# Re-ranking the splitting of weights, and 24 remainders made by accumulating DMAs

## The chip, the cores and the metric

One core of one Trainium2 chip runs the whole program. The metric is the device time of one execution in microseconds (us). Of the kernel before, three executions took 697.01, 698.89 and 701.65 us, so the median is 698.89 us.

## The reference

Two decoder layers over 256 tokens of width 1024, in float32, and a final norm:

```
for layer in range(DEPTH):
    h = rms_norm(x, mix_norm[layer])
    if layer % 2 == 0:
        x = x + gdn_shortconv_mixer(h, ...)
    else:
        x = x + nsa_mixer(h, ...)
    x = x + squared_relu_mlp(rms_norm(x, mlp_norm[layer]), w_up[layer], w_down[layer])
return rms_norm(x, final_norm)
```

The first mixer projects `h` to q, k, v (each 512 wide, then a causal convolution of width 4 and SiLU), z, a, b and three short-convolution parts of 512 (b_gate, c_gate, hs). Its two outputs, the gated delta rule over chunks (`y_a`) and the gated convolution (`y_b`), go side by side into one output projection of 1024 x 1024. The second mixer is block-sparse attention. Each layer ends in an MLP of 1024 x 4096 x 1024.

## The kernel before

**Split weights.** Every large product is made of TensorE products in the type float32r. A weight `w` is split into a high part `uh` (ScalarE: a copy of `w` to float32r) and a remainder `ul = w - uh` (VectorE: a subtraction). Activations are split in the same way, and one tile of a product takes three matmuls: high x high, high x remainder, remainder x high (`mm256`). Weights come from HBM in slots `st` of 128 x 2048 (SyncE issues the loads; four slots). A slot holds two units of 128 x 1024; a unit takes 24 matmuls of 256 columns. There are four buffers each for `uh` and `ul`, so unit i can be split only when unit i-4 has been used. The function `splits` does it, as two streams, one for the even units and one for the odd. A slot is filled anew when both its units are split.

**Units.** Units 0 to 7 are the projection k, 8 to 15 are z, a and b (128 x 512 and 128 x 528), 16 to 19 v, 20 to 23 q, 24 to 27 c_gate, 28 to 31 hs, 32 to 35 b_gate, 36 to 43 the first mixer's output projection. The MLPs and the second mixer follow.

**The first mixer's chain.** After k is convolved (`preconv`, `cvconv`, `K` on VectorE), a chain of small steps follows: the norms of k (`s`, `rk`, `rqt`), `nbk`, `KB`, the scores `al`, the inversion of the chunk's triangle (`lc`, `tt`, `uc`, `ys`, TensorE and VectorE in turn), the two solves (`x`), the outputs (`o`, with GpSimd and ScalarE helping) and `ya`, the second half of the output projection's input. The other half is `yb`. TensorE does the units' matmuls between the steps of the chain. GpSimd makes the mask products `gt`, the convolution of q (`cvpool`, `tap`) and that of the short channel (`CG`).

**The order.** All operations are issued through a wrapper (line 294), so nearly every row of the profile bears L294; the DMA loads bear L426, and instructions are told apart by tile names. A planner written into the kernel (`Order`) simulates the engines with costs and picks at each step the stream that can start first; equal starts go by the stream's rank, the smaller first. A chain has rank 0 or 1, the main stream of matmuls 9, the splits `SPLIT`. What it picks becomes the fixed order of instructions on each engine. A wait in that order holds back what stands behind it on its engine.

Of the kernel before, what the change touches and what calls it, by code (L numbers as in the profile page):

```python
# [10 lines left out]
F32 = mybir.dt.float32  # L11
F32R = mybir.dt.float32r
# [20 lines left out]
PK, PW, PR, F1, GZ, ZP, LD, RT, P2 = 1, 0, 1, 1, 1, 1, 1, 21, 8  # L33
KPOOL, VPOOL, CVB = (), (), {'conv': 4, 'pool': 2}
CHAIN, TOK_FIRST = 0, False
TICK, BUSY = 10240 / 3, 1500.0
MAIN, SPLIT, SHARE, LIMIT, FLOOR, CAP, SPARE = 9, 0, 0.5, 300, -1500.0, 4000.0, 1
ORDER1 = ('kk', 'q0', 'kc', 'vg', 'cmp', 'q1', 'wo')


# [116 lines left out]
class Order:  # L157
# [28 lines left out]
    def flag(self, name):  # L186
        self.flags.setdefault(name, self._now())
# [14 lines left out]
    def spend(self, eng, cost, cols=0.0, port=False):  # L202
# [18 lines left out]
        self.free[eng] = c.t - self.OVER[eng]  # L221
        c.last = eng

    def _next(self, s, value):
        prev, self.cur = self.cur, s
        try:
            s.want = s.gen.send(value)
        except StopIteration:
            self.streams.remove(s)
        self.cur = prev  # L230
# [19 lines left out]
    def run(self):  # L250
        while self.streams:
            best = None
            for i, s in enumerate(self.streams):
                t, at = self._start(s)
                prio = -1 if s.prio == MAIN and self.debt > self.limit else s.prio
                if t is not None and (best is None or (t, prio, i) < best[0]):
                    best = (t, prio, i), s, at
            assert best, [s.want for s in self.streams]
            _, s, at = best
            w, value = s.want, None  # L260
            if isinstance(w, (str, dict)):
                value = at
            else:
                s.hold = max(s.hold, at)
                if w[0] == 'bank':
                    slot = min(self.banks)
                    self.banks.remove(slot)
                    value = self.get_bank(slot[1])
                    self.held[id(value)] = slot[1], value
                elif w[0] == 'take':  # L270
                    self.tokens[w[1]].remove(min(self.tokens[w[1]]))
            self._next(s, value)
# [11 lines left out]
class Timed:  # L284
# [14 lines left out]
    def cost(self, op, a, k):  # L299
        aps = [x for x in list(a) + list(k.values()) if isinstance(x, bass.AP)]  # L300
        size = lambda x: int(np.prod(x.shape[1:]))
        if self.name != 'PE':
            return self.other(op, a, k, aps, size)
        rows = aps[1].shape[0]
        if op == 'transpose':
            return 0.85 * rows, rows * rows / 128
        m, n = size(aps[1]), size(aps[2])
        if aps[2].dtype == F32:
            if m <= 64 and aps[0].start_partition():
                return 8 + 0.7 * m, 0.0  # L310
            return max(1.75 * m, 1.68 * n), 4 * n * rows / 128
        return max((0.86 if aps[2].dtype == F32R else 0.25) * m, 0.46 * n), n * rows / 128

    def other(self, op, a, k, aps, size):
        n = max(size(x) for x in aps)
        if 'dma' in op:
            return 60.0,
        col = any(size(x) == 1 for x in aps[2:]) and n > 1
        sbuf = sum(x.space != PSUM and size(x) > 1 for x in aps[1:])
        if self.name == 'V':  # L320
            if op == 'reciprocal':
                return 150 + 6.4 * n,
            if op == 'memset':
                return 58 + 0.8 * n, 0.0, True
            if op in ('tensor_copy', 'tensor_scalar'):
                quick = sbuf == 1 and aps[0].space != PSUM
                return 150 + (0.55 if quick else 1.06) * n + 60 * col, 0.0, quick
            return 155 + 1.05 * n + 60 * col, 0.0, sbuf > 1 and op not in ('transpose', 'stream_shuffle', 'tensor_reduce')
        if self.name == 'G':
            if op == 'memset':  # L330
                return 90 + 0.9 * n,
            if op in ('tensor_scalar', 'tensor_copy'):
                return 145 + 1.2 * n,
            col = any(list(x.ap)[-1][0] == 0 for x in aps)
            return 180 + (1.68 if col else 2.12) * n,
        need = TABLES.get(a[2] if op == 'activation' else None)
        swap = 0.0
        if need and self.order.table not in need:
            self.order.table, swap = need[0], 1283.0
        return (swap + (150 if aps[1].space == PSUM else 188) + 0.85 * n + 95 * isinstance(k.get('scale'), bass.AP)  # L340
                + 190 * ('accum_out' in k)),
# [26 lines left out]
def _build(ctx, nc, tc, wts, xin, parin, out, off):  # L368
# [86 lines left out]
    def splits(first):  # L455
        for i in range(first, len(units), 2):
# [7 lines left out]
            lo = unitp.tile([128, UN + 64], F32R, name=f"ul{i % UB}")[:, :UN]  # L464
            yield 'A'
            A.activation(hi[:, :n], src, AF.Copy)
            yield 'V'
            V.tensor_sub(lo[:, :n], src, hi[:, :n].bitcast(F32))
            made[i] = hi, lo
            slot = place[p][0]  # L470
            left[slot] -= 1
            if not left[slot]:
                flag(f'st{slot}')
            flag(f'u{i}')

    def unit(keep=1):

# [1383 lines left out]
```

## Time and profile before

| | |
|---|---|
| median of 3 executions | 698.89 us |
| the profiled execution | 699.36 us |
| its span, first to last instruction | 697.6 us |
| mean granted TensorE clock | 0.981 of full |
| TensorE busy (PE) | 664.7 us |
| VectorE busy (DVE) | 479.5 us |
| ScalarE busy (ACT) | 388.1 us |
| GpSimd busy (POOL) | 136.2 us |

PE is TensorE's matmuls, PEld its weight loads, SP the engine that issues loads. Matmuls are pipelined and their ends are modelled. PEclk is the granted clock of TensorE, 1.00 for 2.4 GHz and 0.50 for 1.2 GHz. The first mixer ends at some 180 us of the span.

### The profile page before, as it was taken

To read this page: it belongs to the slowest core of one execution; us is meant where nothing else is said; L and a number is where in the kernel's file an instruction comes from. 1 tells how busy PE (TensorE), PEld (TensorE's weight loads), DVE (VectorE), ACT (ScalarE), POOL (GpSimd) and SP (SyncE) were. 2 spreads that over 40 slices of the span, in tenths; PEclk is the share of its full clock that TensorE was granted. 3 is DMA by queue.
4 is the path that set the end of the run, shared out by engine and by line. 5 is a ranking of instruction groups with operands and counts; after the bars stand their busy time and mean duration, and the time that the engine had idled before them with its cause. 6 is when DMAs were issued, how large, how long until landed. Compare 5 with 4: busy or idle time off the path is not lost.

```text
span 697.6 us, 15854 instructions
## 1 busy us (share of the span) xinstructions
PE 664.7 (95%) x6573; PEld 625.0 (90%) x6573; DVE 479.5 (69%) x898; ACT 388.1 (56%) x750; POOL 136.2 (20%) x177
## 2 busy tenths in 40 slices
PE   8998879996999999999999999999899999999994
PEld 6997779996999999999999876978699999999994
DVE  6999868674775556566568999997396655555452
ACT  7556223331588787444446567676478878544430
POOL 2035678100210000011013251212130000011121
PEclk9999989997999999999999999999999999999997
DMA  8843331311355555555553367213135555555501
GB/s 296 289 175 136 122 123 64 107 36 55 138 206 190 183 189 203 209 185 182 190 207 110 129 224 290 73 62 122 61 122 182 183 183 195 207 201 182 182 1 60
DMA packets 17640, 109.05 MB, mean 156 GB/s; under 512 B 2080, under 2 KB 2336, under 8 KB 5536
## 3 DMA queue, kind: packets, MB, share of 16 engines
q1 hardware_dynamic: 17280, 107.52, 44.1%
q8 instruction: 51, 0.84, 0.5%
q10 hardware_dynamic: 288, 0.52, 0.2%
q14 instruction: 21, 0.17, 0.1%
HBM read 106.99 MB, written 1.05 MB: 155 GB/s over the span
## 4 chain that ended last, share of the span: by engine, by line
PE 75%; DVE 16%; issue 3%; ACT 3%; DMA 1%; SPq 0%; POOL 0%; DVEq 0%; ACTq 0%; POOLq 0%
PE b L294 75%; DVE ul L294 4%; DVE cvconv L294 1%; DVE x L294 1%; ACT uh L294 1%; DVE kc L294 1%; DMA X<-xt 1%; DVE swq L294 1%; DVE rqt L294 1%; DVE X L294 1%; DVE nm L294 0%; ACT px L294 0%; DVE lc L294 0%; DVE qr L294 0%; DVE cm L294 0%
## 5 line engine op out<-in xcount | busy, mean ns | idle before, releaser
L294 DVE TENSOR_TENSOR ul<-st,uh 128x1024 fp32r<-128x1024 f32 (+3 forms) x204 | 244.2, 1200 | 143.4 <-ACT uh L294 141.1
L294 ACT ACTIVATE uh<-st 128x1024 fp32r<-128x1024 f32 (+3 forms) x204 | 205.8, 1011 | 195.3 <-PE b L294 179.6
L294 PE MATMUL b<-x,uh 128*128 128x256 f32 (+1 forms) x1632 | 295.5, 283 | 2.0 <-DVE x L294 0.8
L294 PEld LDWEIGHTS b<-x,uh 128*128 128x128 f32 x1632 | 249.4, 189 | 6.6 <-ACT uh L294 1.8
L294 PE MATMUL b<-x,ul 128*128 128x256 f32 x832 | 231.1, 279 | 0.7 <-DVE ul L294 0.6
L294 PE MATMUL b<-U,uh 128*128 128x256 f32 x1024 | 174.2, 276 | 0.0
L294 PEld LDWEIGHTS b<-x,ul 128*128 128x128 f32 x832 | 157.1, 189 | 1.8 <-DVE ul L294 1.5
L294 PEld LDWEIGHTS b<-U,uh 128*128 128x128 f32 x1024 | 154.1, 188 | 0.0
L294 PE MATMUL b<-U,ul 128*128 128x256 f32 x512 | 141.3, 276 | 0.0
L294 PEld LDWEIGHTS b<-U,ul 128*128 128x128 f32 x512 | 96.1, 188 | 0.0
L294 POOL TENSOR_TENSOR nacc<-nacc,sq 128x256 f32<-128x256 f32 x24 | 27.1, 1127 | 244.2 <-ACT sq L294 244.1
L294 ACT ACTIVATE px<-b,nm 128x128 f32<-128x128 f32 (+1 forms) x64 | 26.3, 423 | 10.0 <-DVE nm L294 9.7
L294 ACT ACTIVATE U<-u 128x256 fp32r<-128x256 f32 x64 | 26.8, 419 | 2.0
L294 ACT ACTIVATE u<-t 128x256 f32<-128x256 f32 x64 | 26.7, 418 | 2.0
L294 POOL TENSOR_TENSOR px<-px,den 128x128 f32<-128x128 f32 x32 | 17.3, 568 | 53.5 <-DVE den L294 39.1
L294 DVE TENSOR_TENSOR U<-u,U 128x256 fp32r<-128x256 f32 x64 | 27.0, 425 | 0.7 <-ACT U L294 0.7
L294 PE MATMUL b<-uh,x 128*128 128x264 f32 (+1 forms) x128 | 24.9, 290 | 0.0
L294 POOL TENSOR_TENSOR X<-X,par 128x256 f32<-128x256 f32 x8 | 5.5, 694 | 99.2 <-ACT nacc L294 90.2
L294 PE MATMUL b<-ohl,uh 128*128 128x256 f32 x128 | 24.6, 291 | 0.2
L294 ACT ACTIVATE t<-b 128x256 f32<-128x256 f32 x64 | 23.3, 364 | 0.0
L294 DVE SCALAR_TENSOR_TENSOR x<-X,par,x 128x256 fp32r<-128x256 f32 x32 | 19.1, 616 | 4.2 <-ACT x L294 4.1
L294 PEld LDWEIGHTS b<-ohl,uh 128*128 128x128 f32 x128 | 19.6, 189 | 0.9 <-ACT ohl L294 0.3
(274 smaller groups left out, 806.0 us busy)
## 6 DMA issues: line engine op xcount, KB each, us to landing
st<-wts SPq DMA_DIRECT2D x94, 1024.0 KB, 4.8
st<-wts SPq DMA_DIRECT2D x4, 560.0 KB, 3.7
st<-wts SPq DMA_DIRECT2D x4, 528.0 KB, 4.8
st<-wts SPq DMA_DIRECT2D x8, 256.0 KB, 5.4
X<-xt SPq DMA_DIRECT2D x3, 256.0 KB, 5.4
par<-par SPq DMA_DIRECT2D x1, 525.0 KB, 5.8
out_dram<-X SPq DMA_DIRECT2D x2, 256.0 KB, 2.6
out_dram<-X ACTq DMA_DIRECT2D x2, 256.0 KB, 3.1
```

The costliest lines, as they stand in the source:

```text
L294: r = f(*a, **k)
```

## The change

Two things. First, `SPLIT` goes from 0 to 0.5: where a split and an operation of a rank 0 chain can start at the same time, the chain's now stands first. Some planner costs of matmuls change a little, and the cost of a DMA issued from GpSimd is now 1000 ns in its table. Second, for units 20 to 43 (24 of 128 x 1024) the remainder is no longer a VectorE subtraction: ScalarE writes `ul = -uh`, and a DMA issued from GpSimd adds `w` from the slot into `ul`, which gives the same value. Whoever uses the unit or refills the slot waits for that DMA. The planner counts it as 3000 ns after the issue.

```
+BYDMA, DLAT = range(20, 44), 3000
+YIELD = (0.0, 0.0, 0.0)
-MAIN, SPLIT, SHARE, LIMIT, FLOOR, CAP, SPARE = 9, 0, 0.5, 300, -1500.0, 4000.0, 1
+MAIN, SPLIT, SHARE, LIMIT, FLOOR, CAP, SPARE = 9, 0.5, 0.5, 300, -1500.0, 4000.0, 1
...
+    def later(self, ns):
+        self.cur.t += ns
+        self.cur.last = None
...
-        return max((0.86 if aps[2].dtype == F32R else 0.25) * m, 0.46 * n), n * rows / 128
+        return max((0.885 if aps[2].dtype == F32R else 0.25) * m, (0.443 if n <= 256 else 0.455) * n), n * rows / 128
...
-            return 60.0,
+            return 1000.0 if self.name == 'G' else 60.0,
...
             A.activation(hi[:, :n], src, AF.Copy)
-            yield 'V'
-            V.tensor_sub(lo[:, :n], src, hi[:, :n].bitcast(F32))
             made[i] = hi, lo
...
+            if i in BYDMA:
+                yield 'A'
+                A.activation(lo[:, :n], hi[:, :n].bitcast(F32), AF.Copy, scale=-1.0)
+                spawn(refill(i, lo[:, :n], src), SPLIT)
+            else:
+                yield 'V'
+                V.tensor_sub(lo[:, :n], src, hi[:, :n].bitcast(F32))
+                split_done(i)
+
+    def refill(i, lo, src):
+        yield 'G'
+        G.dma_start(lo.bitcast(F32), src, accum_op=OP.add)
+        order.later(DLAT)
+        split_done(i)
+
+    def split_done(i):
+        slot = place[units[i][0]][0]
+        left[slot] -= 1
+        if not left[slot]:
+            flag(f'st{slot}')
+        flag(f'u{i}')
```

`YIELD` is zero throughout, so it alters nothing. In the changed file the wrapper's line is 302.

**VectorE where the convolution of k begins.** `ul_303`, `ul_305`, `ul_357` are the remainders of units 8, 9 and 10; `preconv` and `cvconv` are the convolution of k. Before:

```order
L294 TENSOR_TENSOR ul_303<-st,uh_302 128x528
L294 TENSOR_TENSOR ul_305<-st,uh_304 128x528
L294 TENSOR_TENSOR ul_357<-st,uh_356 128x528
L294 MEMSET preconv 128x4
L294 TENSOR_TENSOR preconv<-b_104,rbc 128x256
```

and with the change, from behind unit 9's remainder on:

```order
L302 MEMSET preconv 128x4
L302 TENSOR_TENSOR preconv<-b_105,rbc 128x256
L302 TENSOR_SCALAR cvconv<-preconv,par 128x256 x2
L302 SCALAR_TENSOR_TENSOR cvconv<-preconv,par,cvconv 128x256 x6
L302 MEMSET preconv 128x4
L302 TENSOR_TENSOR preconv<-b_106,rbc 128x256
L302 SCALAR_TENSOR_TENSOR K<-K,cvconv 128x256 x2
L302 TENSOR_SCALAR cvconv<-preconv,par 128x256
L302 MEMSET preconv 128x4
L302 TENSOR_TENSOR preconv<-b_107,rbc 128x256
L302 SCALAR_TENSOR_TENSOR cvconv<-preconv,par,cvconv 128x256
L302 TENSOR_SCALAR cvconv<-preconv,par 128x256
L302 SCALAR_TENSOR_TENSOR cvconv<-preconv,par,cvconv 128x256 x4
L302 TENSOR_TENSOR ul_357<-st,uh_356 128x528
```

Unit 10's remainder now stands behind four `preconv` with their memsets (the first pair stands just ahead of these rows), 15 `cvconv` and two `K`.

**VectorE ahead of the norms of k.** `s` and the first `rk` begin the chain. Before, where the last remainder ahead of them is unit 22's:

```order
L294 SCALAR_TENSOR_TENSOR g<-sp,ea 128x16
L294 CAST gp_683<-g 128x16
L294 TENSOR_TENSOR gp_684<-g,gp_683 128x16
L294 TENSOR_TENSOR ul_696<-st,uh_695 128x1024
L294 SCALAR_TENSOR_TENSOR cvconv<-preconv,par,cvconv 128x256
L294 TENSOR_SCALAR s_743<-b_618 128x16
L294 TENSOR_SCALAR rk<-s_743 128x16
```

With the change, where it is unit 17's:

```order
L302 TENSOR_TENSOR ul_434<-st,uh_433 128x528
L302 TENSOR_TENSOR ul_447<-st,uh_446 128x528
L302 TENSOR_TENSOR ul_466<-st,uh_465 128x528
L302 TENSOR_TENSOR ul_482<-st,uh_481 128x528
L302 TENSOR_TENSOR ul_503<-st,uh_502 128x1024
L302 TENSOR_TENSOR ul_525<-st,uh_524 128x1024
L302 TENSOR_SCALAR s_550<-b_455 128x16
L302 TENSOR_SCALAR rk<-s_550 128x16
```

The remainders of units 18 to 22, the decay's small steps (`lw` to `gp`) and a part of v's convolution no longer stand ahead of the chain on VectorE.

**GpSimd at the mixer's end.** `o` is the chain's output, `ul` the output projection's remainders. Before:

```order
L294 TENSOR_TENSOR CG<-CG,rbc 128x256 x2
L294 TENSOR_TENSOR o_2313<-o_2313,gz_635 128x512
L294 TENSOR_TENSOR o_2470<-o_2470,gz_652 128x512
L294 TENSOR_TENSOR nacc<-nacc,sq 128x256 x12
```

With the change:

```order
L302 DMA ul_2111<-st 128x1024
L302 TENSOR_TENSOR o_2166<-o_2166,gz_627 128x512
L302 DMA ul_2224<-st 128x1024
L302 DMA ul_2320<-st 128x1024
L302 DMA ul_2382<-st 128x1024
L302 TENSOR_TENSOR o_2412<-o_2412,gz_648 128x512
L302 DMA ul_2445<-st 128x1024
L302 DMA ul_2476<-st 128x1024
L302 DMA ul_2520<-st 128x1024
L302 DMA ul_2553<-st 128x1024
```

All eight of the output projection's remainders (units 36 to 43) are issued by GpSimd, between and behind the two products of `o`.

## Rows read from the trace of the kernel before

**Rows 1.** Busy time by stage of the program, the stretches in us of the span; the columns are PE, PEld, DVE, ACT and POOL busy us with instructions, granted clock, share of the DMA engines, GB/s.

```profile
40.00:100.00 60.00, 50.68 (x677) 47.08 (x678) 52.28 (x116) 23.05 (x38) 37.03 (x39) 0.95 0.32 111
100.00:160.00 60.00, 60.00 (x1300) 55.42 (x1298) 42.73 (x100) 19.52 (x31) 20.83 (x26) 0.99 0.27 91
160.00:180.00 20.00, 14.59 (x91) 13.44 (x91) 8.71 (x18) 3.99 (x5) 1.26 (x1) 0.74 0.15 52
180.00:370.00 190.00, 189.62 (x1664) 188.75 (x1663) 120.46 (x161) 119.31 (x198) 14.57 (x19) 1.00 0.55 189
370.00:510.00 140.00, 135.07 (x1025) 111.04 (x1024) 117.58 (x285) 89.45 (x257) 38.93 (x64) 1.00 0.37 130
510.00:697.60 187.60, 177.43 (x1552) 176.21 (x1551) 104.47 (x140) 107.49 (x177) 19.24 (x20) 0.98 0.44 158
```

**Rows 2.** The same view of the two stretches in which the clock was low, and of one in which TensorE had nothing but units.

```profile
94.50:101.30 6.80, 6.25 (x132) 5.68 (x134) 2.80 (x4) 1.89 (x3) 5.42 (x7) 0.50 0.16 22
166.10:176.40 10.30, 6.87 (x29) 6.20 (x30) 4.00 (x12) 1.64 (x3) 0.02 (x1) 0.50 0.26 88
30.00:40.00 10.00, 10.00 (x90) 10.00 (x88) 10.00 (x22) 6.25 (x11) 0.00 (x0) 1.00 0.92 347
```

**Rows 3.** What matmuls waited for between 40 and 180 us: who waited for whom, us in total, times, longest us.

```profile
PE b L294 <- DVE o L294: 4.6, 1, 4.6
PE b L294 <- issue: 2.5, 1, 2.5
PE b L294 <- DVE ys L294: 1.9, 1, 1.9
PE b L294 <- DVE preconv L294: 1.5, 1, 1.5
PE b L294 <- DVE tt L294: 1.4, 1, 1.4
```

**Rows 4.** The matmuls in order of time at the mixer's end: start us, us, what.

```profile
163.85 0.28 PE L294 MATMUL b<-yb,ul 128*128 128x256 f32 x1
168.70 1.08 PE L294 MATMUL b<-par,o 128*128 128x128 f32 x4 [4.58 <-DVE o L294]
170.47 1.31 PE L294 MATMUL b<-ya,uh 128*128 128x256 f32 x2 [0.69 <-ACT ya L294]
```

**Rows 5.** VectorE in order of time around the norms of k, in the same columns.

```profile
45.08 2.06 DVE L294 TENSOR_TENSOR ul<-st,uh 128x1024 fp32r<-128x1024 f32 x1
47.07 1.26 DVE L294 SCALAR_TENSOR_TENSOR cvconv<-preconv,par,cvconv 128x256 f32<-128x256 f32 x1
48.25 0.16 DVE L294 TENSOR_SCALAR s<-b 128x16 f32<-128x16 f32 x1
...
52.23 2.35 DVE L294 TENSOR_TENSOR ul<-st,uh 128x1024 fp32r<-128x1024 f32 x2
54.50 1.01 DVE L294 SCALAR_TENSOR_TENSOR nbk<-beta,rk 128x16 f32<-128x16 f32 x1
```

**Rows 6.** Groups of VectorE's and ScalarE's instructions by shape, 40 to 172 us and 40 to 180 us: count, busy us, mean ns of one, idle us before them. The last row is the busy time from 40 to 100 us of the instructions on `uh` alone, in the columns PE, PEld, DVE (the remainders), ACT.

```profile
L294 DVE TENSOR_TENSOR ul<-st,uh 128x1024 fp32r<-128x1024 f32 x23 | 31.6, 1377 | 7.2 <-ACT uh L294 7.2
...
L294 ACT ACTIVATE uh<-st 128x1024 fp32r<-128x1024 f32 x24 | 25.3, 1056 | 53.0 <-PE b L294 46.0 <-issue 7.0
...
40.00:100.00 60.00, 35.84 (x186) 29.87 (x187) 18.70 (x13) 12.66 (x12) 0.95 0.32 111
```

**Rows 7.** VectorE in order of time where the convolution of k begins.

```profile
19.70 1.95 DVE L294 TENSOR_TENSOR ul<-st,uh 128x528 fp32r<-128x528 f32 x3
21.58 0.42 DVE L294 TENSOR_TENSOR preconv<-b,rbc 128x256 f32<-128x256 f32 x1
21.92 0.42 DVE L294 TENSOR_TENSOR preconv<-b,rbc 128x256 f32<-128x256 f32 x1
22.25 0.61 DVE L294 TENSOR_SCALAR cvconv<-preconv,par 128x256 f32<-128x256 f32 x2
23.39 1.27 DVE L294 SCALAR_TENSOR_TENSOR cvconv<-preconv,par,cvconv 128x256 f32<-128x256 f32 x3
26.61 0.42 DVE L294 SCALAR_TENSOR_TENSOR K<-K,cvconv 128x256 f32<-128x256 f32 x1
```

**Rows 8.** TensorE in order of time: the first matmul of unit 8, and the pair with which unit 9 ends (the 24 of the two units follow each other).

```profile
20.16 0.37 PE L294 MATMUL b<-uh,x 128*128 128x264 f32 x1
22.89 0.40 PE L294 MATMUL b<-uh,x 128*128 128x264 f32 x2
```

**Rows 9.** DMA issues of the whole program: count, KB each, median us from issue to landing; and the loads of slots between 40 and 180 us: the ns that SyncE's issue took, and least, median and longest us to landing.

```profile
st<-wts SPq DMA_DIRECT2D x94, 1024.0 KB, 4.8
st<-wts SPq DMA_DIRECT2D x4, 560.0 KB, 3.7
...
L426 SPq DMA_DIRECT2D st<-wts x12: 328/328/328, 41.5 to 172.7; - x12
...
DMA to landing us min/median/max: 4.8/4.8/5.4
```

**Rows 10.** GpSimd in order of time: the same instruction alone, and beside a VectorE remainder that ran from 77.44 to 78.68 us.

```profile
76.30 0.73 POOL L294 TENSOR_TENSOR cvpool<-cvpool,tap 128x256 f32<-128x256 f32 x1
76.98 0.62 POOL L294 TENSOR_TENSOR tap<-prepool,par 128x256 f32<-128x256 f32 x1
77.68 1.60 POOL L294 TENSOR_TENSOR cvpool<-cvpool,tap 128x256 f32<-128x256 f32 x1
```

**Rows 11.** What the queue of loads waited for between 40 and 180 us.

```profile
SPq L426 <- DVE ul L294: 77.0, 7, 18.0
```

More of the change, by code (lines that the diff above doesn't have):

```diff
@@ L255, in run @@
                 prio = -1 if s.prio == MAIN and self.debt > self.limit else s.prio
-                if t is not None and (best is None or (t, prio, i) < best[0]):
-                    best = (t, prio, i), s, at
+                if t is not None:
+                    key = t + (0.0 if isinstance(s.want, tuple) else YIELD[min(int(prio), 2)]), prio, i
+                    if best is None or key < best[0]:
+                        best = key, s, at
             assert best, [s.want for s in self.streams]
@@ L466, in splits @@
             A.activation(hi[:, :n], src, AF.Copy)
-            yield 'V'
-            V.tensor_sub(lo[:, :n], src, hi[:, :n].bitcast(F32))
             made[i] = hi, lo
[L470 to L474, printed above, removed]
+            if i in BYDMA:
[17 more added lines that the diff above has]
+        flag(f'u{i}')
     def unit(keep=1):
```

## The prediction

> **What bounds the kernel now.** I first read the busy time by stage [rows 1]. From 180 to 370 us the matmuls fill 189.62 of 190 us, and in the last MLP 177.43 of 187.6: there TensorE is the bound, and neither part of the change touches a matmul's count. The time that can be won lies in the first mixer. From 40 to 100 us TensorE idles 60 - 50.68 = 9.3 us while VectorE is busy for 52.28 of 60, and from 160 to 180 us it idles 20 - 14.59 = 5.4 us. From 100 to 160 us it does not idle.
>
> The second view is the same one of the two stretches with a granted clock of 0.50, the lower of the two levels [rows 2]: 6.8 us from 94.5 on and 10.3 us from 166.1 on, both entered after TensorE had idled. Matmuls ran for 6.25 and 6.87 us there, so a full clock would give back at most half, 3.1 and 3.4 us. Idle time and low clock make 9.3 + 5.4 + 3.1 + 3.4 = 21.2 us: the ceiling of what the mixer can give.
>
> Third, who was waited for [rows 3], and the end of the mixer in order of time [rows 4]. The matmuls on `yb` end at 163.85 us, then TensorE stands still for 4.58 us until VectorE's `o` and again 0.69 us until `ya`. So the chain of the delta rule ends last, and the units' matmuls are used up before it. Inside the chain, `ys` and `tt` cost 1.9 and 1.4 us. The chain starts late: VectorE reaches `s` at 48.25 us, behind a remainder of 2.06 us, and `nbk` at 54.50, behind two more [rows 5].
>
> **The change part by part.**
>
> *The chain on VectorE.* By the order, the remainders of units 18 to 22 no longer stand ahead of `s`; the group's mean is 1.38 us [rows 6], so five are 6.9 us. From `s` to the mixer's end all remainders of units 20 to 43 leave VectorE, 23 of them 31.6 us in the stretch of 40 to 172 us [rows 6]. To take away the wait at the end the chain must come 4.58 + 0.69 = 5.3 us earlier against the matmuls, and it comes earlier by 6.9 us before `nbk` is even reached. So I count the end as won: -5.4 us of idle time and -3.4 us of low clock, **-8.8 us**. Bounds: 0, if something else ends the chain, and -8.8.
>
> *40 to 100 us.* Here VectorE is the bound; 13 of the 23 remainders lie in this stretch, 18.7 us [rows 6] of its 52.28. With these gone TensorE should be fed. What stays are the inversion's own turns between the engines, `ys` and `tt`, 1.9 + 1.4 = 3.3 us [rows 3]. I take 9.3 + 3.1 - 3.3 = 9.1, **-9.1 us**; bounds -12.4 and, if only a third comes, -4.
>
> *A new wait early.* Unit 10's remainder now stands behind four `preconv`, 15 `cvconv` and two `K`. By their durations [rows 7]: 4 x 0.34 (from start to start), 4 x 0.30, 11 x 0.42 and 2 x 0.42 make 8.0 us. Before, that remainder was the third in the group of 1.95 us, from 21.0 to 21.6 us; now it ends near 21.0 + 8.0 + 0.65 = 29.7 us. TensorE's work on units 8 and 9 runs from 20.16 to 23.3 us [rows 8]. So it stands still for some 6.4 us, where before it had 90 matmuls in 10 us [rows 2] and no gap to give. I take **+6 us**. Whether the clock falls after it is open: the falls of [rows 2] followed idle stretches of this size, and one costs 0 to 3.4 us; I take **+1.7 us**.
>
> *ScalarE.* 24 negations of the same shape as `uh`, 1.056 us each [rows 6], 25.3 us, on an engine that is busy 23.05 + 19.52 of 120 us there [rows 1]. Cover: its idle time. Without it, a chain step behind a negation waits 1 us. I take 0.
>
> *GpSimd.* 24 issues, whose duration the trace does not show. The nearest rows are SyncE's issue of 0.33 us [rows 9] and a GpSimd instruction that met a VectorE one, 1.60 us [rows 10]: 8 to 38 us in all, on an engine that is busy 37.03 + 20.83 of 120 us [rows 1]. Behind them stand `gt`, `cvpool` and `CG`; each issue also waits for ScalarE's negation. The scores of k need the `gt`; the q convolution is needed only by the chain's end. I take 0, with up to +3 us kept for the range.
>
> *The remainder's way.* With four buffers a unit goes round once in four units' time. A unit takes 24 matmuls, at 90 in 10 us [rows 2] 2.67 us, so four take 10.7 us. In that time lie `uh` (1.06), the negation (1.06), the DMA's issue and landing (L), and the unit's own matmuls (2.67). So L may be 10.7 - 4.8 = 5.9 us before TensorE waits; beyond that each unit pays (L - 5.9)/4. From 100 to 160 us the chain's small matmuls fill in, so only about 20 units pay: some 12 before the inversion and the last eight, of the output projection. L is not in the trace. From below: issue 0.33 us and landing 3.7 us, as for a load of 560 KB [rows 9], 4.0. From above: issue 1.6 us and, if the destination has to be read too, the longest landing of a load of twice the bytes, 5.4 us [rows 9], 7.0. The row nearest in size is the 560 KB load, that nearest in traffic the 1024 KB one; between, L = 5.5 us, **0 us**. At 7.0 it would be 20 x 1.1/4 = +5.5 us.
>
> *Loads and bandwidth.* SyncE refills a slot when the later of its two remainders has landed, no longer at VectorE's subtraction, for which it waited 77.0 us [rows 11]. Four slots are eight units, 21 us; load, splits and DMA take about 4.8 + 4 x 1.06 + 5.5 = 14.5, so this stays hidden. 24 x 0.52 MB over some 130 us are 96 GB/s, 192 if the destination's reading counts, beside 91 to 111 [rows 1]; with 303 at most it is under the 347 GB/s that the rows reach [rows 2].
>
> *Attention.* The ranks also reorder the second mixer. TensorE idles 140 - 135.07 = 4.9 us there [rows 1]; I take 0, with 3 us to both sides.
>
> *Sum.* -8.8 - 9.1 + 6 + 1.7 = -10.2 us. The profiled execution took 699.36 us (a span of 697.6 and 1.8 around it), 0.5 over the median. 699.4 - 10.2 - 0.5 gives 688.7; I say **688**. The forecast's own range is 681 to 696.
>
> **The rivals.**
>
> *All of it.* The early stall is covered and the whole ceiling comes: 699 - 21 = 678. For it: VectorE was busy without a gap from 30 to 40 us [rows 2] and loses more than the ceiling. Against it: the eight us ahead of unit 10's remainder are in the order itself.
>
> *A slow DMA makes it slower.* The place is the ring of four buffers in the stretches that are nothing but units, above all the output projection, whose eight DMAs stand one behind the other on GpSimd. At the price of 20/4 = 5 us for each us of L over 5.9, the gain of 10.2 is gone at L = 7.9, and the time is over 706 from L = 9.3 on. With two 1024 KB landings and an issue, 9.6 + 1 = 10.6, it is 699 - 10.2 + 23.5 = 712. For it: nothing in the trace shows an accumulating DMA, and it must read two things for each that it writes. Against it: all 12 loads here land in 4.8 to 5.4 us [rows 9].
>
> *No change.* The new wait takes the place of the old: early stall and low clock in full, 6.4 + 3.4 = +9.8, and only a third in the middle, -8.8 - 4 + 9.8 = -3, so 696. For it: the order puts the stall there for certain; the chain has many turns between engines that no remainder delays.
>
> *GpSimd is held up by VectorE.* The same `cvpool` addition took 0.73 us alone and 1.60 beside a remainder [rows 10], 0.87 longer. If an issue is held in this way, once or twice, L grows from 5.5 to 6.4 or 7.2, and the time by 2.5 to 6.7 us: 691 to 695. The Trainium skill, "SBUF — State Buffer", section "SBUF: two separate sides", goes further: VectorE can lock GpSimd out of the port through which it writes a DMA's descriptors, and the page gives 3100 ns beside such work for a DMA of 620 ns alone. By that figure L would grow by 2.5 us to 8.0, and the sum would end, as an estimate from the page, at 699 instead of 688. The page ties this to VectorE's two-port modes and, for two-input work, to a GpSimd that reads SBUF, so a subtraction need not hold an issue; no row here shows a DMA from GpSimd.
>
> **How the numbers follow.** Chances: forecast 0.45, all of it 0.15, slow DMA 0.15, no change 0.15, GpSimd held up 0.10. About 1% of 699, or 7 us, is what a measurement can tell from no change. Faster than 692: three quarters of the forecast (0.34), all of "all of it" and a third of "held up": 0.53. Slower than 706: the slow DMA and a little of the others, 0.17. Within: 0.30. The range takes in the better case and most of the rest: 675 to 705; beyond it lie the slow DMA (above) and the largest gains, 2 in 10 together.
>
> **What would show it.** Right: no wait for `o` of several us at the mixer's end, no low clock there, `s` reached before 45 us, VectorE under 45 us busy from 40 to 100 us; and a stall of TensorE of 5 to 7 us from 23 us on. DMAs from GpSimd that land within 6 us of their issue's start. Wrong: landings of 8 us or more, TensorE waiting for DMA into `ul` in many units; GpSimd busy throughout from 45 us with `cvpool` or `CG` late; or the first matmuls on `ya` no earlier than 170 us [rows 4].

## The result, and the profile after

The change is slower: 708.3 us (median of ten runs) against 697.9 us (ten runs of the kernel before on the same chip), a ratio of 1.0115 with a 95% interval of 1.0082 to 1.0148. The forecast was 688 us. The profiled execution of the change took 707.46 us, with a span of 705.6. Four of the ten runs show a lower mean clock (0.960 to 0.962, the others 0.969 to 0.979) and took 714.5 to 714.9 us: the medians in this document hold such runs, the ratios leave them out.

Lines of that execution's page: the engines' busy time, the two queues that move data, q1 for the loads and q0 for GpSimd's DMAs (packets, MB, share of 16 engines), GpSimd's new instruction, and DMA issues (count, KB, median us to landing).

```profile
PE 668.4 (95%) x6573; PEld 631.3 (89%) x6573; DVE 445.7 (63%) x870; ACT 415.2 (59%) x781; POOL 142.1 (20%) x198
...
q1 hardware_dynamic: 17280, 107.52, 44.2%
q0 software_dynamic: 3456, 12.58, 9.3%
...
L302 POOL DMA_DIRECT2D ul<-st x24 | 21.2, 894 | 68.8 <-DVE lw L302 29.6
...
ul<-st POOLq DMA_DIRECT2D x24, 512.0 KB, 5.9
```

9.3% of the span over 24 transfers is 9.3% x 705.6 / 24 = 2.73 us of all 16 engines for 512 KB. For the loads, 44.2% over 107.52 MB make 3.04 us for 1024 KB.

The busy time by stage, in the columns of [rows 1], and below it two of its stretches of low clock.

```profile
40.00:100.00 60.00, 55.80 (x962) 52.33 (x961) 41.79 (x122) 36.56 (x51) 30.23 (x38) 0.99 0.88 222
100.00:160.00 60.00, 58.25 (x1039) 54.08 (x1038) 28.59 (x85) 26.38 (x39) 30.78 (x43) 0.95 0.69 169
160.00:180.00 20.00, 17.17 (x141) 16.52 (x140) 8.33 (x17) 11.72 (x12) 4.70 (x5) 1.00 0.83 196
180.00:200.00 20.00, 15.30 (x119) 15.10 (x120) 13.34 (x18) 9.53 (x17) 4.57 (x5) 0.83 0.55 180
...
30.40:33.90 3.50, 3.03 (x14) 3.03 (x15) 3.33 (x7) 1.80 (x5) 0.00 (x0) 0.51 0.18 35
...
180.60:187.50 6.90, 3.14 (x14) 3.14 (x15) 1.17 (x3) 0.52 (x2) 0.00 (x0) 0.51 0.44 118
```

VectorE fell from 52.28 to 41.79 us between 40 and 100 us and TensorE rose from 50.68 to 55.80 [rows 1]: the relief came. But the DMA share went from 0.32 to 0.88, and at the mixer's end, where TensorE idled 5.4 us from 160 to 180 us [rows 1], it now idles 2.8 us there and 4.7 in the 20 us after.

TensorE in order of time, the three longest waits of the span (start us, us, what, idle us before it and its releaser).

```profile
30.87 0.59 PE L302 MATMUL b<-ul,x 128*128 128x264 f32 x1 [5.48 <-DVE ul L302]
...
184.36 0.58 PE L302 MATMUL b<-ya,ul 128*128 128x256 f32 x1 [6.85 <-DMA ul<-st]
...
406.28 0.57 PE L302 MATMUL b<-uh,x 128*128 128x280 f32 x1 [2.63 <-DVE t L302]
```

The first is unit 10's remainder, as forecast. The second is new: nothing waits for `o` any more [rows 4], but the last remainder of the output projection lands at 184.3 us. GpSimd issued it at 172.95 us, 0.08 us behind a load of 1024 KB, and from 168 to 180 us the DMA engines had no time left (the row below, in the columns of [rows 1]). The third lies in the second mixer. Then the remainders' DMAs as GpSimd issues them, ns least/median/longest, and us to landing; last the loads of slots between 40 and 180 us in the same way.

```profile
168.00:180.00 12.00, 9.17 (x76) 8.59 (x74) 3.16 (x4) 6.17 (x7) 1.72 (x2) 1.00 1.01 214
...
L302 POOL DMA_DIRECT2D ul<-st x24: 852/868/1284, 49.3 to 172.9; - x24
...
DMA to landing us min/median/max: 4.5/5.9/11.4
...
L434 SPq DMA_DIRECT2D st<-wts x13: 327/328/328, 41.5 to 172.9; - x13
...
DMA to landing us min/median/max: 4.7/6.5/9.0
```

The chain after: VectorE's first step `s` and its last on `o` (duration in ns, then the start), and the first matmul on `ya` (start, us).

```profile
L302 DVE TENSOR_SCALAR s<-b x1: 175/175/175, 41.4 to 41.4; 128x16 f32<-128x16 f32 x1
...
L302 DVE TENSOR_TENSOR o<-o,ors x1: 696/696/696, 167.3 to 167.3; 128x512 f32<-128x512 f32 x1
...
170.56 0.38 PE L302 MATMUL b<-ya,uh 128*128 128x256 f32 x1
```

Before, they start at 48.25 [rows 5], 167.9 and 170.47 us [rows 4]. The chain starts 7 us earlier and ends where it ended. TensorE does not wait for `o` because it still has matmuls on `yb`: the last starts at 170.3 us, before at 163.85 [rows 4].

To see where time goes in all the runs, I use two marks of each trace: when the first matmul on `U` starts (the first mixer and the start of its MLP lie ahead of it) and the time from there to the last one (the second mixer lies in between).

```profile
L302 PE MATMUL b<-U,uh x1024: 276/276/276, 279.7 to 693.9; 128*128 128x256 f32 x171
L302 PE MATMUL b<-U,ul x512: 276/276/276, 279.9 to 694.0; 128*128 128x256 f32 x171
```

Before, these are 273.7 us and 412.4 us; after, 279.7 and 414.3. So the first mixer lost 6.0 us and the second 1.9.

| run | median us | ratio to before, same chip | 95% | first U | to last U |
|---|---|---|---|---|---|
| change | 708.3 | 1.0115 | 1.0082–1.0148 | 279.7 | 414.3 |
| e1 ranks, new numbers | 703.5 | 1.0055 | 1.0027–1.0082 | 277.2 | 415.2 |
| e2 DMAs, no ranks | 703.4 | 1.0069 | 1.0032–1.0107 | 277.9 | 415.9 |
| e3 16 DMAs | 703.2 | 1.0029 | 0.9990–1.0068 | 271.3 | 414.2 |
| e4 small addition | 701.0 | 1.0014 | 0.9975–1.0053 | 270.9 | 413.9 |
| e5 new numbers alone | 716.8 | 1.0268 | 1.0241–1.0295 | 287.2 | 415.4 |
| e6 ranks, old numbers | 698.8 | 1.0013 | 0.9988–1.0039 | 274.9 | 413.7 |
| e7 change, old numbers | 707.2 | 1.0137 | 1.0099–1.0175 | 280.2 | 412.3 |
| e8 late ranks, 16 DMAs | 709.1 | 1.0153 | 1.0131–1.0176 | 280.7 | 418.0 |
| e9 plain copy | 695.1 | 0.9945 | 0.9914–0.9976 | 267.3 | 414.2 |
| e10 early ranks alone | 704.7 | 1.0083 | 1.0052–1.0114 | 278.8 | 412.7 |
| e11 unit 10 excepted | 713.0 | 1.0189 | 1.0139–1.0239 | 286.3 | 416.9 |
| e12 every other unit | 707.6 | 1.0127 | 1.0085–1.0169 | 271.4 | 422.6 |
| e13 small copy | 698.7 | 0.9995 | 0.9972–1.0018 | 269.8 | 414.1 |
| e14 small addition again | 701.1 | 1.0024 | 0.9991–1.0057 | 272.6 | 414.2 |
| e15 late ranks | 700.4 | 1.0013 | 0.9994–1.0031 | 268.8 | 417.6 |
| e16 units 16 to 43 | 695.7 | 0.9964 | 0.9929–0.9998 | 268.8 | 413.0 |
| e17 units 20 to 43 | 696.2 | 0.9947 | 0.9921–0.9973 | 268.7 | 413.9 |
| e18 the same, 8 DMAs | 692.7 | 0.9910 | 0.9884–0.9935 | 265.4 | 413.6 |

The marks are of one profiled execution each; the first also holds the kernel's first loads, which differ by a microsecond or two (the median landing of three pieces of `X` was 5.4 us before and 7.0 in the change's). The profiled execution of e3 (699.0 us) is 4 us under its median and that of e2 (707.6) 4 us over.

### The profile page after: what moved, and what is told of

Read it like the earlier page. It is cut to its first block, busy times and chain, and to the rows that moved or that the text cites. A ratio compares the mean times of both kernels' runs of the same rounds, so it can differ in the third digit from the quotient of the medians.

```text
span 705.6 us, 15897 instructions
## 1 busy us (share of the span) xinstructions
PE 668.4 (95%) x6573; PEld 631.3 (89%) x6573; DVE 445.7 (63%) x870; ACT 415.2 (59%) x781; POOL 142.1 (20%) x198
## 3 DMA queue, kind: packets, MB, share of 16 engines
q1 hardware_dynamic: 17280, 107.52, 44.2%
## 4 chain that ended last, share of the span: by engine, by line
PE 83%; DVE 8%; DMA 3%; ACT 2%; issue 2%; SPq 0%; DVEq 0%; ACTq 0%
PE b L302 83%; DVE ul L302 2%; DMA ul<-st 2%; DMA X<-xt 1%; ACT uh L302 1%; DVE x L302 1%; DVE cvconv L302 1%; DVE kc L302 1%; DMA st<-wts 1%; DVE X L302 1%; DVE KL L302 0%; DVE swq L302 0%; DVE nm L302 0%; SPq L434 0%; DVE t L302 0%
## 5 line engine op out<-in xcount | busy, mean ns | idle before, releaser
L302 DVE TENSOR_TENSOR ul<-st,uh 128x1024 fp32r<-128x1024 f32 (+3 forms) x180 | 209.6, 1167 | 145.9 <-ACT uh L302 144.1
L302 PE MATMUL b<-x,uh 128*128 128x256 f32 (+1 forms) x1632 | 299.2, 285 | 1.7 <-ACT uh L302 0.8
L302 POOL TENSOR_TENSOR nacc<-nacc,sq 128x256 f32<-128x256 f32 x24 | 28.7, 1195 | 245.4 <-ACT sq L302 245.4
L302 POOL DMA_DIRECT2D ul<-st x24 | 21.2, 894 | 68.8 <-DVE lw L302 29.6
L302 PE MATMUL b<-uh,x 128*128 128x264 f32 (+1 forms) x128 | 30.2, 319 | 3.9 <-DVE t L302 2.6
L302 PEld LDWEIGHTS b<-uh,x 128*128 128x128 f32 x128 | 23.7, 213 | 4.5 <-issue 2.8
L302 PE MATMUL b<-ul,x 128*128 128x264 f32 (+1 forms) x64 | 20.4, 319 | 5.5 <-DVE ul L302 5.5
L302 ACT ACTIVATE ul<-uh 128x1024 fp32r<-128x1024 f32 x24 | 25.2, 1054 | 0.4
```

The lines of the kernel that those rows point to most:

```text
L302: r = f(*a, **k)
```

## The experiments

All edits are against the changed kernel. "The old numbers" are the matmul costs of the planner before:

```diff
-        return max((0.885 if aps[2].dtype == F32R else 0.25) * m, (0.443 if n <= 256 else 0.455) * n), n * rows / 128
+        return max((0.86 if aps[2].dtype == F32R else 0.25) * m, 0.46 * n), n * rows / 128
```

The first four kernels take the change apart. The first expectation states three theories of the loss, A, B and C.

**e1, re-ranking without DMAs.**

```diff
-BYDMA, DLAT = range(20, 44), 3000
+BYDMA, DLAT = (), 3000
```

> All 44 remainders are VectorE subtractions again, ranked 0.5 as in the change: re-ranking alone, with no accumulating DMA. Theory A (the DMAs are the loss: they fill the DMA engines and land late, re-ranking would gain): the wait for the DMA into ul at 177 us (6.8 us) and the low clock behind it (3.4 us at most) have no cause left, the early wait for unit 10's remainder (5.5 us) stays; 685 to 695 us against 698 of the kernel before. Theory B (the re-ranking is the loss: the early wait, the clock falls behind waits of the chain, the second mixer's 2.6 us wait): 700 to 710 us. Theory C (the place of the 24 issues and negations on GpSimd and ScalarE is the loss, not the transfers): as A, 685 to 695; e4 tells A from C.

703.5 us, in B's range, but only half of the loss: slower than before without a single DMA, and by the ratios 0.6%, 4 us, faster than the change. The wait at the mixer's end is gone, the early one and the second mixer's 2.6 us stay.

**e2, DMAs without re-ranking.**

```diff
-MAIN, SPLIT, SHARE, LIMIT, FLOOR, CAP, SPARE = 9, 0.5, 0.5, 300, -1500.0, 4000.0, 1
+MAIN, SPLIT, SHARE, LIMIT, FLOOR, CAP, SPARE = 9, 0, 0.5, 300, -1500.0, 4000.0, 1
```

> The 24 accumulating DMAs with rank 0 for the splitting, so without the re-ranking. Theory A: the same 12.6 MB cross the DMA engines and land in 5 to 11 us, so units wait for DMA into ul; 703 to 715 us, and no wait for unit 10's remainder near 25 us. Theory B: without the re-ranking the DMAs cost nothing and take VectorE's work away; 688 to 698 us. Theory C: as A.

703.4 us, as theory A has it, but not by its mechanism: one wait for DMA into `ul` of 2.1 us, and 5.9 us for `o` at the mixer's end. The wait in the second mixer is there without the ranks, which speaks against B.

**e3, the output projection's remainders back on VectorE.**

```diff
-BYDMA, DLAT = range(20, 44), 3000
+BYDMA, DLAT = range(20, 36), 3000
```

> As the change, but the output projection's eight remainders (units 36 to 43) are VectorE subtractions; 16 DMAs stay. Theory A, with the loss at the mixer's end (6.8 us of wait and up to 3.4 us of low clock there): 697 to 702 us, no wait for DMA into ul after 160 us. Theory A with the loss spread over 54 to 110 us, the end being late for that reason: 704 to 708. Theory B: within 2 us of the change, 706 to 710.

703.2 us, between A's two cases; by the ratios 0.9%, 6 us, faster than the change. In the profiled executions the first `U` comes 8.4 us earlier than in the change, and after 160 us nothing waits for a DMA. So most of the loss by DMAs sits in the output projection's eight; how much the other 16 cost e3 does not show.

**e4 (and e14), the traffic taken away.**

```diff
-        G.dma_start(lo.bitcast(F32), src, accum_op=OP.add)
+        G.dma_start(lo[:, :64].bitcast(F32), src[:, :64], accum_op=OP.add)
```

> The change's own program and order, but each of the 24 DMAs moves and adds only the first 64 columns of a unit; the remainders of the other columns are left out (they hold minus the high part). Instructions, waits and issues stay, one eighth of the accumulating traffic is left. Theory A: DMAs land in 3 to 5 us and loads in about 5, the wait at 177 us and the clock fall behind it go; 692 to 700 us. Theory B: still 706 to 710. Theory C: still 704 to 710, since issues, negations and their order are the same.

701.0 us, first `U` 8.8 us earlier than in the change. Issues, negations and their order are the same, so theory C falls. Landings, from the trace of e4:

```profile
DMA to landing us min/median/max: 2.1/2.3/5.4
```

With C gone and both A and B half right, the third part of the change came under suspicion, the planner's new numbers (theory D), with the early wait.

**e5, the new numbers alone** (no DMAs, rank 0).

```diff
-BYDMA, DLAT = range(20, 44), 3000
+BYDMA, DLAT = (), 3000
-MAIN, SPLIT, SHARE, LIMIT, FLOOR, CAP, SPARE = 9, 0.5, 0.5, 300, -1500.0, 4000.0, 1
+MAIN, SPLIT, SHARE, LIMIT, FLOOR, CAP, SPARE = 9, 0, 0.5, 300, -1500.0, 4000.0, 1
```

> Only the third, smallest part of the change: the planner's new numbers for a matmul's time (0.885 for 0.86, 0.443 and 0.455 for 0.46); splitting at rank 0, all remainders on VectorE. With the old numbers that program is instruction for instruction the kernel before. Theory D (these numbers reorder the second mixer, and the waits there of 2.6 us for t and 1.7 us for px with the low clock behind them come from them): both waits near 400 us as in the kernels run so far, U to the last U about 2 to 3 us longer than the 412.4 us of before; 700 to 703 us against 698. Theory B (the re-ranking makes them): no such waits near 400 us, 697 to 699.

716.8 us, far over either. What matmuls waited for from 150 to 200 us, and the stage at the mixer's end, in e5's trace:

```profile
PE b L302 <- DVE o L302: 6.8, 2, 6.6
```

```profile
160.00:180.00 20.00, 14.39 (x104) 12.93 (x103) 6.50 (x15) 3.00 (x5) 0.69 (x1) 0.50 0.00 1
```

By other estimates of a matmul the planner spends the units' matmuls earlier (513 matmuls instead of 677 from 40 to 100 us, in about the same busy time), and the first `U` comes 13.5 us later, with the whole stage at the mixer's end at the low clock. Theory D is right on the second mixer (415.4 us, waits of 2.7 and 1.7 us there) and far too small in all.

**e6, re-ranking with the old numbers** (no DMAs).

> The re-ranking alone with the planner's old numbers for a matmul. Theory D with the early wait: the wait of 5.5 us near 24 us and the clock fall behind it stay, some of it is won back by the chain's earlier start, no 2.6 us wait near 400 us; 698 to 701 us. Theory B: as with re-ranking and the new numbers together, 702 to 705.

698.8 us, as D has it: neither faster nor slower. Two stretches and the stage from 40 us, in e6's trace:

```profile
118.00:128.00 10.00, 10.00 (x182) 9.18 (x182) 6.41 (x21) 4.65 (x8) 5.93 (x9) 1.00 0.31 108
128.00:138.00 10.00, 10.00 (x71) 9.15 (x71) 4.55 (x9) 0.00 (x0) 4.99 (x6) 0.50 0.00 0
...
40.00:100.00 60.00, 50.62 (x1085) 47.07 (x1085) 51.34 (x124) 21.98 (x35) 18.90 (x21) 0.91 0.37 125
```

The chain's matmuls move ahead (1085 matmuls instead of 677 in that stage), TensorE is no busier, and the end of the mixer is fed. What that wins goes into the early wait and into more time at the low clock.

**e7, the whole change with the old numbers.**

> The whole change but for the planner's numbers for a matmul, which are the old ones. Theory D: 2 to 5 us under the change, 703 to 706 us, with no 2.6 us wait near 400 us; landings of the accumulating DMAs as before, median about 6 and at most 11 us. Theory B: no difference, 707 to 710.

707.2 us, in B's range by the time; but the second mixer is back at 412.3 us without the wait there, as D has it, and the first mixer is no shorter (280.2). Within the change the numbers cost 2 us in the second mixer and nothing that I can measure in all.

**e8, all three suspected losses out:** the old numbers, `range(20, 36)` as in e3, and rank 0 ahead of unit 18, by a line at the head of the loop in `splits`:

```diff
+            order.cur.prio = SPLIT if i >= 18 else 0
```

> All three suspected losses taken out at once: the old numbers for a matmul, rank 0.5 only from unit 18 on (so unit 10's remainder stands where it stood before), and 16 accumulating DMAs (units 20 to 35) instead of 24. If the early wait (5.5 us and up to 3.4 of low clock), the second mixer (2 us) and the end of the mixer (6.8 and up to 3.4) are losses of their own (theories A, D and the early wait): no wait near 24 us, none over 2 us near 400 us, 686 to 693 us, faster than both kernels. If the early wait only moves (TensorE's units used up at one time or another, since the chain's length sets the mixer's end): 696 to 702.

709.1 us: 16 us over the first case and 7 over the second. Its waits from 40 to 160 us:

```profile
PE b L302 <- issue: 13.4, 5, 5.0
```

The early wait is gone, and the planner has put the chain's steps elsewhere, where TensorE stands still in turn, for nothing that the profile names. Ahead of the first `U` the clock is low for 37.5 us, before for 17.1, and the second mixer is 5.6 us longer, too.

**e9, the same bytes without adding.** The order of all instructions is the change's own.

```diff
-        G.dma_start(lo.bitcast(F32), src, accum_op=OP.add)
+        G.dma_start(lo.bitcast(F32), src)
```

> The change's program and order, but the 24 DMAs copy w over the remainder's tile and add nothing (the remainder is left as w; the subtraction of the high part is left out). The bytes written are the same. Theory A1 (the accumulating is dear: the destination is read as well, 2.7 us of all 16 engines for 512 KB against 1.5 us, half of a 1024 KB load's 3.04): the DMAs hold the engines for 1.5 us each, land in about 3.5 to 4 us, the 6.8 us wait at 177 us goes; 699 to 703 us. Theory A2 (any 512 KB in that place does it, by its bytes or by its issue and landing): 705 to 710 us and landings as in the change, median about 6 us.

695.1 us: theory A1, and better than it said. From the page of e9 and from its view of GpSimd's DMAs:

```profile
q0 software_dynamic: 3456, 12.58, 4.6%
...
L302 POOL DMA_DIRECT2D ul<-st x24 | 13.8, 575 | 71.0 <-DVE lw L302 30.5
```

```profile
DMA to landing us min/median/max: 2.8/3.9/8.4
```

4.6% x 693.3 / 24 = 1.33 us of the 16 engines instead of 2.73: adding doubles the engines' time. It also lengthens the issue, by 894 - 575 = 319 ns. The wait at the mixer's end is gone and that stage runs at full clock. The first matmul on `ya` starts 5.0 us earlier than in the change:

```profile
L302 PE MATMUL b<-ya,uh x64: 276/276/388, 165.6 to 177.2; 128*128 128x256 f32 x64
```

**e10, the early ranks alone** (no DMAs, the old numbers, and `order.cur.prio = 0.5 if i < 18 else 0` in the loop).

> Before's program and numbers, with rank 0.5 for units 0 to 17 alone; all remainders on VectorE, no DMA. It prices the early wait, with only what it brings forward of the chain. If the prediction's price of the early wait holds (5.5 us and 1.7 of clock) and the gain comes from the later ranks: 703 to 706 us, the wait for o at the mixer's end still there. If the early ranks alone start the chain earlier and so pay for the wait: 697 to 700 us, as re-ranking alone with the old numbers, and no wait for o.

704.7 us, 5.7 over before and in the first case's range. It leaves the expectation in one point: there is no wait for `o`, though the first matmul on `ya` starts only at 178.0 us; the middle waits more, and its clock is low for 20.5 us from 40 to 160, before for 6.8. So the 5.7 us are not the early wait alone.

**e11, unit 10 excepted** (as e3, with `order.cur.prio = 0 if i == 10 else 0.5`).

> The change with 16 DMAs (units 20 to 35) and one exception in the ranks: unit 10's remainder keeps rank 0, so it stands ahead of the convolution of k. Beside the run with 16 DMAs and all ranks (median 703, profiled execution 699): if the early wait is a loss by itself, 5.5 to 7 us less: 692 to 697 us, faster than before. If the wait only moves to unit 11 or to the chain, 698 to 704 us.

713.0 us, over both cases. The wait did not go, it moved to unit 11, in e11's trace from 24 to 34 us:

```profile
31.00 0.59 PE L302 MATMUL b<-ul,x 128*128 128x264 f32 x1 [5.99 <-DVE ul L302]
```

That is the second case; the 9 us above its range it does not explain. The clock was low for 37.5 us ahead of the first `U`, as in e8.

**e12, every other unit.**

```diff
-BYDMA, DLAT = range(20, 44), 3000
+BYDMA, DLAT = range(20, 44, 2), 3000
```

> Every other unit from 20 to 42 by DMA, 12 in all, so that no two of them follow one another in the ring and the added traffic is halved; the rest as in the change. Theory A with the engines' throughput as the limit: no wait for DMA into ul, landings near 5 us, 697 to 703 us. If it is the single transfer's way (negation, issue, landing, 6 us and more) that a unit waits for, wherever it stands: waits for ul near the end stay, 704 to 709 us.

In the first mixer theory A holds: 271.4 us, no wait for a DMA into `ul` over 1.1 us. DMAs from GpSimd in e12's trace:

```profile
DMA to landing us min/median/max: 4.4/5.3/7.2
```

The time is 707.6 us all the same, since the second mixer takes 422.6 us, with waits for `px` of 3.6 and for `t` of 2.6 us. It holds none of the DMAs; its order has changed with the rest.

**e13 and e14, 64 columns copied or added.** e13 has both edits of e4 and e9: 64 columns, no adding; e14 is e4 once more.

> The change's program and order, but the 24 DMAs copy only the first 64 columns and add nothing (the remainder is left unfinished in all columns). With the change, the plain copy and the small addition it makes a square: adding or not, 512 KB or 32 KB. If only the traffic costs (theory A): as the plain copy or up to 2 us under it, 693 to 696 us, and the small addition in the same call as well. If the accumulating issue on GpSimd (0.89 us instead of 0.58) costs too: 693 to 696 us here and 699 to 702 for the small addition.

> The small addition (64 of the columns; the remainder is left unfinished in the others) once more, beside the small copy on the same chip. Theory A, traffic alone: within 1.5 us of the small copy, 693 to 697 us. If GpSimd's longer issue costs: 4 to 7 us above the small copy, 699 to 702.

0.9995 and 1.0024 of before, with intervals that overlap: GpSimd's longer issue costs nothing or up to 5 us, which these runs can't settle. Nor do they explain why the copy of 512 KB is the fastest of the four (0.9945); its first mixer had 10.2 us at the low clock and theirs 17.1 to 20.5, and the reason stays open. What stands is that the change, at 1.0115, is alone in its loss: adding 512 KB costs 0.9 to 1.7%, 6 to 12 us.

**e15, the late ranks alone** (no DMAs, the old numbers, the line of e8).

> Before's numbers, no DMA, rank 0.5 from unit 18 on and 0 ahead of it: the other half of the re-ranking. With before (698), the early ranks alone (+5.7) and all ranks with the old numbers (+0.7) it closes a second square. If the two halves are independent, the later ranks gain 5 us and the early wait costs 5.7: 691 to 695 us, faster than before, no wait for o at the mixer's end and none near 24 us. If the later ranks gain only because the early ones have brought the chain forward (the early wait is the price of the gain): 697 to 703 us.

700.4 us: by the time the second case, by the marks not. The first mixer is 4.9 us shorter, and the second 5.2 us longer, in another order. So the question was put again with before's order in the second mixer.

**e16 and e17, ranks for the first mixer alone** (no DMAs, the old numbers; e17 with 20 for 16).

```diff
+            order.cur.prio = 0.5 if 16 <= i < 44 else 0
```

> Before's numbers, no DMA, rank 0.5 for units 16 to 43 alone; the second mixer and the MLPs keep rank 0, and VectorE's order there is that of before. With the later ranks for all units the first mixer ended 4.9 us earlier (first U at 268.8 instead of 273.7) and the second mixer gave it back (+5.2 from the first U to the last). If the loss was the second mixer's new order: 692 to 695 us, first U near 269, 412 to 413 us from there to the last U; faster than both kernels. If the first mixer's gain was that order's own chance: 696 to 701.

> The same with units 20 to 43, the second mixer again in before's order: whether the gain hangs on the ranks or on one order that the planner happens to find. The gain is the ranks': 691 to 696 us. It is chance: 697 to 705, with waits between 70 and 110 us in other places.

Both are faster than before, by 0.4 and 0.5% (e16's interval ends at 0.9998), and both times lie between the two cases expected. The stages of e17:

```profile
40.00:100.00 60.00, 49.92 (x943) 46.40 (x941) 50.78 (x125) 20.71 (x37) 28.48 (x30) 0.91 0.29 101
...
160.00:180.00 20.00, 19.39 (x170) 19.20 (x169) 13.52 (x24) 8.84 (x15) 0.87 (x1) 1.00 0.54 193
```

The end of the mixer is fed at full clock, 19.39 instead of 14.59 us; from 40 to 100 us nothing is gained.

**e18, eight spaced DMAs on e17.**

```diff
-BYDMA, DLAT = (), 3000
+BYDMA, DLAT = range(20,36,2), 5000
```

> The version with rank 0.5 for units 20 to 43 (696.2 us, 0.5% under before), and eight accumulating DMAs on top: units 20, 22 to 34, every other one, with 5000 ns for the planner's landing time instead of 3000. They take 8 x 1.38 = 11 us from VectorE where TensorE is busy for only 49.9 of 60 us. If spaced DMAs land in 5 us and VectorE is the bound there: TensorE over 53 us busy from 40 to 100 us, no wait for DMA into ul, 690 to 694 us. If the chain's turns between the engines bound that stretch and not VectorE's load: 40 to 100 us as before, 695 to 698. If the DMAs cost even so: 699 to 704.

692.7 us, 0.9% under before: the fastest version that computes the reference. Its interval overlaps that of e17, so what the eight DMAs add is likely but not shown. Its stages:

```profile
40.00:100.00 60.00, 50.26 (x1078) 46.38 (x1078) 45.40 (x117) 26.70 (x41) 29.33 (x39) 0.94 0.54 143
100.00:160.00 60.00, 58.01 (x893) 54.21 (x893) 41.55 (x104) 23.05 (x35) 23.65 (x31) 1.00 0.35 99
160.00:180.00 20.00, 20.00 (x177) 20.00 (x178) 13.33 (x19) 10.84 (x18) 3.63 (x3) 1.00 0.58 210
```

The time is as the first case expected, the sign is not: TensorE is busy for 50.26 us from 40 to 100 us, not for over 53. VectorE's load is 5 us less there, so that it alone was the bound is not shown. 1078 matmuls instead of 943 lie there, so the chain is ahead: the first matmul on `ya` starts at 165.3 us, in e17 at 168.6. The DMAs landed in 5.8 us at the median and 9.0 at most, and no matmul waited for one.

## Why the prediction was wrong

The step that failed is *the remainder's way*, counted as 0 us, and with it *loads and bandwidth*. Its L was nearly right in the median (5.9 us for 5.5). But it took L as one transfer's length, independent of what else moves, and measured the traffic in GB/s averaged over 130 us, where 303 stayed under 347 [rows 2]. The trace shows the engines' own time: per pair of units one load of 3.04 us and two accumulating transfers of 2.73, 8.5 us, while TensorE needs 2 x 2.67 = 5.3 us for the pair. In the output projection, a stretch of nothing but units, the engines were full from 168 to 180 us. Landings of 8 to 11 us follow, and loads that take 9.0 us instead of 5.4 at most [rows 9]. By the same count the plain copy needs 3.04 + 2 x 1.33 = 5.7 us for a pair and every other unit by DMA 5.8, near TensorE's 5.3, and there no matmul waited for a DMA for more than 1.1 us (e9, e12).

Measured against the kernels with the same order (e9, e13, e14), the term of the DMAs is +6 to +12 us. Some 7 us of it lie at the mixer's end: from the first matmul on `ya` to the first `U` the change takes 109.1 us, e9 101.7 and e4, e13 and e14 102.2 to 102.3. Ahead of that matmul e9 is 5.0 us earlier than the change but e14 only 0.2, so that part stays open. That is the rival "a slow DMA makes it slower", given 0.15; its place, the output projection, was right (e3), and its sum of 712 us is near, though only the last wait of 6.85 us and the low clock behind it show.

*The chain on VectorE*, -8.8 us: right at its start, wrong at its end. `s` starts at 41.4 us instead of 48.25, but at `o` half a microsecond of that lead is left, and the first matmul on `ya` starts at 170.56 us, which the prediction had named as a sign of being wrong. That no matmul waits for `o` comes from matmuls on `yb` that last 6.5 us longer, not from an earlier chain. The same order with plain copies keeps 4.9 us of the lead (e9); where the change loses it the runs do not show. In e17 the end is fed although `s` starts at 49.4 us. In the change the new wait takes the place of the old. From 160 to 200 us TensorE idled 5.8 us before [rows 1] and 7.5 after; the matmuls at the low clock fell from 6.87 us [rows 2] to 3.14, half of which is lost: 9.2 against 9.1 us. The term came to 0.

*40 to 100 us*, -9.1: 5.1 us less idle time, and the low clock down from 5.5 us of the stage to 1.3, worth half, 2.1: -7.2 us. The ranks alone bring nothing there (e6, e17), so it needs the DMAs. That VectorE's load was the bound, as said, is not shown: in e18 VectorE is busy for 45.40 us there instead of 50.78, and TensorE for 50.26 instead of 49.92. But 1.8 us of idle time and some 2 of low clock came back from 100 to 160 us, where the prediction had no term.

*A new wait early*, +6 and +1.7: 5.48 us, and 3.4 at the low clock behind it, worth at most 1.7. Right; the falls of [rows 2] had come in shorter waits than this one, of 4.6 and 2.5 us [rows 3]. That it could be taken out on its own was an error of mine in the experiments: e8 and e11 moved it.

*Attention*, 0 within 3 us: +1.9, from the planner's numbers (e7), not from the ranks, as the prediction had it. That the numbers were no part of the sum at all was a gap: alone they cost 2.7% (e5). The change hides this, for with the ranks (e1) or the DMAs (e2) most of it is gone.

*GpSimd*: 0.87 us an issue at the median and 1.28 at the longest, within the estimate of 0.33 to 1.6. *GpSimd held up by VectorE*: not seen. The Trainium skill, "SBUF — State Buffer", section "SBUF: two separate sides", gives 3100 ns for a GpSimd DMA beside a VectorE `tensor_copy`, 620 alone. Here VectorE was busy for 41.79 of 60 us from 40 to 100 us, mostly with instructions of other kinds, and no issue took over 1.28 us; no run here shows the page's case.

By the sum: early +7.2, 40 to 100 us -7.2, 100 to 160 us +3.9, end 0, second mixer +1.9, and the first loads about +1.6 (a difference that executions of other kernels show too) make +7.4, where the spans differ by 8.0.

## What to carry to other kernels

Price a DMA by the time it takes of the engines, beside the loads of the same stretch, not by its latency alone or by mean GB/s; an accumulating one took as much as a load of nearly twice its bytes. When a planner sets the order, any new number in it is a change of its own: measure it alone, and mark each stage's end, because a gain in one stage was eaten by another order in the next (e12, e15). What ends a wait must be asked again once it is gone: here the chain's wait of 4.6 us was replaced by a DMA's of 6.9. And a wait that is gone does not show that what it waited for came earlier; look up both times, for here the waiting engine had become later.

## What the hardware showed that I had not expected

Adding makes a copy between two tiles cost twice the DMA engines' time (2.73 and 1.33 us for 512 KB), and the issue on GpSimd half as long again (0.87 and 0.59 us at the median).

The clock also fell without idle time of TensorE that the profile shows ahead of it (the ends of matmuls are modelled). In e6 it was at the full level from 118 to 128 us and at the lower from 128 to 138, with TensorE busy for 10.00 of 10 us in both; ahead of the fall 34 of its 182 matmuls were the units', the others the chain's small ones between them. In e6 the clock is 0.91 on average from 40 to 100 and from 100 to 160 us, against 0.95 and 0.99 before [rows 1]; but the change, with the same ranks, other numbers and the DMAs, has 0.99 and 0.95. What in the mix of matmuls brings it about these runs do not show.
